# Keeping the expert gates of the last two token quarters on chip, and pinning the stores of the first two between the chunks

## The chip, the cores and the metric

One core of a Trainium2 chip (trn2) runs the whole program. The metric is the device time of one execution in microseconds; the time of a kernel is the median of its runs.

## The reference, cut to what matters

The program computes three transformer blocks over 256 tokens of width 1024. The change lies in the last sublayer, a product-key mixture of 16,384 experts (128 x 128):

```python
def _peer(h, w_query, sub_keys, expert_u, expert_v):
    q = (h @ w_query).reshape(B, S, PEER_HEADS, 2, PEER_KEY_DIM)
    sc = jnp.einsum('bshpk,hpnk->bshpn', q, sub_keys).astype(jnp.float32)
    v1, i1 = lax.top_k(sc[..., 0, :], PEER_TOPK)
    v2, i2 = lax.top_k(sc[..., 1, :], PEER_TOPK)
    ...
    top_s, pos = lax.top_k(cand, PEER_TOPK)
    idx = jnp.take_along_axis(cand_idx, pos, axis=-1)
    g = jax.nn.softmax(top_s, axis=-1).astype(h.dtype)
    ...
        u = expert_u[it]
        act = jax.nn.gelu(jnp.einsum('td,tkd->tk', xt, u))
        return jnp.einsum('tk,tkd->td', gt * act, expert_v[it])
```

Each token chooses 8 x 16 experts, each with a gate `g`. The reference gathers the rows of the chosen experts; the kernel does not gather.

## The kernel before

The kernel treats the sublayer densely: it computes the Gelu activation of all 16,384 experts for all 256 tokens, multiplies it with a gate matrix that is zero where an expert was not chosen, and multiplies the product with `expert_v`. An expert's number is 128 x its first key + its second; `n2` (0 to 127) is one second key, and a tile for one `n2` has the 128 first keys on the partitions and the 256 tokens along the free dimension.

The stages of `peer` around the change:

- `up(n2)` loads a slab of `expert_u` (512 KB, `raw`, by SP), splits it into a high part (`wH`, ScalarE, L268) and a rest (`wL`, VectorE, L270), runs 24 matmuls into a PSUM tile `acc` (two of these exist), and evicts it through Gelu on ScalarE (L1414), for most `n2` into a tile `gs`, which SP stores to a DRAM tensor `spill` (L1416); for the others into a kept tile `ga`. The `up` calls are independent of the routing and serve as filler for TensorE: `fill` issues them from a list while the routing and the gate build run.
- The gate build turns the chosen numbers and gates into the dense gate matrix, a quarter of the tokens (TQ = 64) at a time, four quarters, each in eight chunks of TC = 8 tokens. For a chunk VectorE makes one-hot tiles `A`, `eqb` and `Bg`, TensorE multiplies them (`gb`, 16 short matmuls, L1553), and ScalarE copies the result into `G` (L1554), a tile of 128 x 128 x 64 f32, 32 KB a partition, in two buffers. After a chunk, one store of the quarter before is popped from a list (`stores`), and `fill(2.8)` follows.
- A store writes an eighth of a quarter's `G` (512 KB) to the DRAM tensor `gd`, issued from ScalarE's queue (L1561, 32 in all). The stores of the last quarter follow between the remaining `up` calls.
- The expert loop runs over the 128 `n2`: `gates_of` loads gates of four `n2` from `gd` into `GG` (L1579, 512 KB, from SP, two groups ahead), VectorE multiplies activation and gate (`gw`, L1589), ScalarE and VectorE split the product (`gaH`, L1593; `gaL`, L1594), and 12 matmuls accumulate with the two parts of a slab of `expert_v` into four PSUM banks (`v`). Activations that were spilled are loaded back into `ga` (L1610).

The order of instructions on each engine is made by a planner, which simulates the program and issues what is ready first, in the order of priority in which the program was written; each engine then runs its list in order. `tc.keep_in_program_order(ins)` gives the planner an edge that puts `ins` behind the instruction written just before it on the same engine. SP issues nearly all loads; ScalarE issues the `gd` stores.

Of the kernel before, what the change touches and what calls it, by code (L numbers as in the profile page):

```python
# [11 lines left out]
F32 = mybir.dt.float32  # L12
# [5 lines left out]
AF = mybir.ActivationFunctionType  # L18
OP = mybir.AluOpType
# [200 lines left out]
def program(ctx: ExitStack, tc, I, out, co):  # L220
    nc = tc.nc
# [85 lines left out]
    def tables(name):  # L307

        tc.keep_in_program_order(nc.scalar.preload_act_table_set(name))
# [1062 lines left out]
    NQ = T // TQ  # L1372
# [6 lines left out]
    def peer(Xq, done):  # L1379
# [11 lines left out]
        X = normed(xt, 8, r, lambda k: cc("norm_ffn", k), pair())  # L1391
        pre.close()
        with pool("peer") as mp, pool("psp", 2, space=PS) as ps:
            iT = [mp.tile([128, T], F16 if j < 2 else F32, name=f"iT{j}") for j in range(3)]
            gp = [mp.tile([128, T], F16, name=f"gp{j}") for j in range(2)]
            iota = mp.tile([128, 128], F16, name="iota")
# [133 lines left out]

            done()

            gd = dram.tile([NQ, 128, 128, TQ], F32, name="gd")
            stores = []
            with pool("build") as bt, pool("psb", space=PS) as pb:
                for q in range(NQ):
                    G = bt.tile([128, 128, TQ], F32, name="G", bufs=2)
                    for c in range(TQ // TC):
                        A = bt.tile([128, TC, 128], F16, name="A", bufs=2)
                        B = bt.tile([128, TC, 2, 128], F16, name="Bg", bufs=2)  # L1540
                        s = slice(TQ * q + TC * c, TQ * q + TC * c + TC)
                        inner = lambda v: v[:, s, None].to_broadcast([128, TC, 128])
                        numbers = iota[:, None, :].to_broadcast([128, TC, 128])
                        eq = bt.tile([128, TC, 128], F16, name="eqb", bufs=1)
                        nc.vector.tensor_tensor(A, numbers, inner(iT[0]), op=OP.is_equal)
                        nc.vector.tensor_tensor(eq, numbers, inner(iT[1]), op=OP.is_equal)
                        for i in range(2):
                            nc.vector.tensor_tensor(B[:, :, i], eq, inner(gp[i]), op=OP.mult)
                        for j in range(0, TC, TP):
                            p = pb.tile([128, TP, 128], F32, name="gb", bufs=4)  # L1550
                            for k in range(TP):
                                for i in range(2):
                                    nc.tensor.matmul(p[:, k], A[:, j + k], B[:, j + k, i], start=i == 0, stop=i == 1)  # L1553
                            nc.scalar.activation(G[:, :, TC * c + j:TC * c + j + TP], p.rearrange("p t n -> p n t"), AF.Copy,  # L1554
                                                 scale=2.0 ** -15)
                        if stores:
                            stores.pop(0)()
                        fill(2.8)

                    def store(q, G, n):  # L1560
                        return lambda: nc.scalar.dma_start(gd[q, :, n:n + SN], G[:, n:n + SN])  # L1561

                    stores += [store(q, G, n) for n in range(0, 128, SN)]
                for n2 in todo:
                    up(n2)
                    if stores:
                        stores.pop(0)()
                while stores:
                    stores.pop(0)()
            with pool("psv", space=PS) as pv:  # L1570
                acc = [[pv.tile([128, 512], F32, name=f"v{t}{n}") for n in range(2)] for t in range(2)]
                with pool("gates") as gt:
                    parts = {}

                    def gates_of(i):

                        if i < 128 // GN:
                            parts[i] = gt.tile([128, NQ, GN, TQ], F32, name="GG", bufs=3)
                            dma(parts[i], gd[:, :, GN * i:GN * i + GN].rearrange("q n a t -> n q a t"))  # L1579

                    gates_of(0)
                    gates_of(1)
                    ends = []
                    for n2 in range(128):
                        h, j = divmod(n2, GN)
                        if j == 0:
                            gates_of(h + 2)
                        w = gt.tile([128, T], F32, name="gw", bufs=2)
                        nc.vector.tensor_tensor(w.rearrange("p (q t) -> p q t", q=NQ), ga.pop(n2).rearrange("p (q t) -> p q t", q=NQ),  # L1589
                                                parts[h][:, :, j], op=OP.mult)  # L1590
                        aH = gt.tile([128, T], F32R, name="gaH", bufs=2)
                        aL = gt.tile([128, T], F32R, name="gaL", bufs=2)
                        nc.scalar.activation(aH, w, AF.Copy)  # L1593
                        nc.vector.tensor_sub(aL, w, aH)  # L1594
                        H, L = slab(I["v"][n2])
                        ends.append((n2, (aH, aL), (H, L)))
                        if n2 == 126:
                            continue

                        order = (tc.keep_in_program_order,) if n2 == 127 else ()  # L1600
                        for t in range(2):
                            for n in range(2):
                                for m, a, b in ends:
                                    mm3(acc[t][n], [v[:, 128 * t:128 * t + 128] for v in a],
                                        [v[:, 512 * n:512 * n + 512] for v in b], m == 0, m == 127, *order)
                        ends.clear()
                        nxt = n2 + AHEAD
                        if nxt < STASH:
                            ga[nxt] = mp.tile([128, T], F32, name="ga", bufs=AHEAD)
                            dma(ga[nxt], spill[nxt - AHEAD])  # L1610
                        elif nxt < 128:
                            up(nxt)
                tables(LOGEXP)
                with pool("fin") as gt:
                    nf = gt.tile([128, D], F32, name="nf")
                    dma(nf, bass.AP(tensor=I["norm_final"].tensor, offset=I["norm_final"].offset, ap=[[0, 128], [1, D]]))
                    cs = [slice(512 * n, 512 * n + 512) for n in range(2)]
                    ss = [gt.tile([128, 2], F32, name="ss", bufs=2) for _ in range(2)]
                    rs = [gt.tile([128, 1], F32, name="rf", bufs=2) for _ in range(2)]
                    ys = [gt.tile([128, D], F32, name="y", bufs=2) for _ in range(2)]  # L1620
                    kept = tc.keep_in_program_order

                    def add(t, n):
                        xs = xtok[:, t, cs[n]]
                        kept(nc.vector.tensor_add(xs, acc[t][n], xs))
                        sq = gt.tile([128, 512], F32, name="sqf", bufs=2)
                        nc.scalar.activation(sq, xs, AF.Square, scale=D ** -0.5, accum_out=ss[t][:, n:n + 1])

                    def gain(t):
                        kept(nc.vector.tensor_mul(ys[t][:, cs[0]], xtok[:, t, cs[0]], nf[:, cs[0]]))  # L1630

                    def total(t):
                        kept(nc.vector.tensor_add(rs[t], ss[t][:, 0:1], ss[t][:, 1:2]))

                    def put(t, n):

                        kept(nc.vector.scalar_tensor_tensor(ys[t][:, cs[n]], xtok[:, t, cs[n]], rs[t], nf[:, cs[n]],
                                                            op0=OP.mult, op1=OP.mult))
                        dma(out[0, 128 * t:128 * t + 128, cs[n]], ys[t][:, cs[n]])

                    add(0, 0)
                    add(0, 1)
                    add(1, 0)
                    total(0)
                    gain(1)
                    add(1, 1)
                    rsqrt(rs[0], rs[0], gt, kept)
                    total(1)
                    put(0, 0)
                    put(0, 1)  # L1650
                    rsqrt(rs[1], rs[1], gt, kept)
                    nc.scalar.activation(ys[1][:, cs[0]], ys[1][:, cs[0]], AF.Copy, scale=rs[1])
                    dma(out[0, 128:, cs[0]], ys[1][:, cs[0]])
                    put(1, 1)
# [71 lines left out]
```

## Time and profile before

| | us |
|---|---|
| median of three timed runs | 2041.73 |
| lowest and highest of them | 2039.51, 2043.0 |
| the profiled execution, its own time | 2036.42 |
| its span, first to last instruction | 2034.6 |
| TensorE busy (PE) | 1933.5 (95%) |
| VectorE busy (DVE) | 1561.7 (77%) |
| ScalarE busy (ACT) | 1160.6 (57%) |
| GpSimd busy (POOL) | 116.0 (6%) |
| mean granted clock of TensorE, share of full speed | 0.975 |

The profile is of one execution. Its names: PE is TensorE, PEld its weight load, DVE VectorE, ACT ScalarE, SP the engine that only issues transfers; ACTq and SPq are the issue queues of ScalarE and SP. A line such as L1414 is the line of the kernel that issued the instruction; `out<-in` names its tiles. Times count from the start of the span. In this span the gate build runs from about 1389 to 1629 us, the hand-over to the expert loop until about 1669, the loop until about 2022, and the final normalization until the end.

### The profile page before, as it was taken

The page shows a single profiled execution, that of the slowest core. Times are in us where ns is not written, and L with a number is a line of the kernel's source. Part 1 is how long each engine was busy: PE and PEld are TensorE (multiplying, and loading weights), DVE is VectorE, ACT ScalarE, POOL GpSimd, SP SyncE. Part 2 cuts the span into 40 slices and gives each one's busy share as a digit, 9 for nine tenths or more (in the row PEclk, how much of TensorE's full clock was granted, in tenths as well). Part 3 has the DMA queues.
Part 4 walks back from the last instruction along what each step waited for, and adds up shares of the span by engine and source line. Part 5 has one row for each costly group of instructions (what it writes and reads, how often), then busy time and mean ns, then how long its engine had stood idle before and what let it go on. Part 6 is the DMA issues. An engine that isn't in the chain of part 4 may idle for free.

```text
span 2034.6 us, 36363 instructions
## 1 busy us (share of the span) xinstructions
PE 1933.5 (95%) x13516; PEld 1748.0 (86%) x13516; DVE 1561.7 (77%) x3040; ACT 1160.6 (57%) x2196; POOL 116.0 (6%) x139
## 2 busy tenths in 40 slices
PE   7988999989999999999999999999999989999998
PEld 6755899878888887999987999999999978888886
DVE  8877986466876877765687589999889847777676
ACT  5644586445775675774476464555444535555554
POOL 0000122120111102001000010000000000000000
PEclk9988999989999999999999999999999989999999
DMA  9775778676646535755643555556776688888774
GB/s 361 262 238 184 249 215 242 218 250 227 206 134 223 173 126 170 221 181 186 237 146 113 177 178 177 175 180 200 265 260 219 227 302 294 283 295 286 229 239 140
DMA packets 172434, 441.91 MB, mean 217 GB/s; under 512 B 21104, under 2 KB 75144, under 8 KB 171616
## 3 DMA queue, kind: packets, MB, share of 16 engines
q1 hardware_dynamic: 154608, 397.41, 59.4%
q10 hardware_dynamic: 11808, 36.70, 5.0%
q0 software_dynamic: 5840, 5.47, 1.1%
q8 instruction: 106, 1.74, 0.4%
q14 instruction: 72, 0.59, 0.1%
HBM read 398.40 MB, written 37.91 MB: 214 GB/s over the span
## 4 chain that ended last, share of the span: by engine, by line
PE 72%; DMA 12%; DVE 8%; issue 3%; ACT 3%; ACTq 1%; SPq 0%; POOL 0%; DVEq 0%; POOLq 0%
PE acc L275 16%; PE acc L276 16%; PE acc L277 16%; PE v L275 6%; PE v L276 6%; PE v L277 6%; DMA bias_d<-ob 5%; DMA araw<-in_adaT 4%; DVE wL L270 2%; DVE araw L465 1%; PE gb L1553 1%; ACTq L1561 1%; PE S L953 1%; DMA br<-buck_d 1%; ACT wH L268 1%
## 5 line engine op out<-in xcount | busy, mean ns | idle before, releaser
L270 DVE TENSOR_TENSOR wL<-raw,wH 128x1024 fp32r<-128x1024 f32 x565 | 695.0, 1232 | 242.5 <-ACT wH L268 224.4
L268 ACT ACTIVATE wH<-raw 128x1024 fp32r<-128x1024 f32 x565 | 596.9, 1059 | 489.3 <-PE acc L276 320.7
L275 PE MATMUL acc<-hH,wH 128*128 128x256 f32 (+1 forms) x2168 | 628.4, 290 | 29.4 <-ACT gs L1414 20.0
L276 PE MATMUL acc<-hL,wH 128*128 128x256 f32 (+1 forms) x2168 | 619.8, 286 | 3.2 <-DVE hL L394 3.2
L277 PE MATMUL acc<-hH,wL 128*128 128x256 f32 (+1 forms) x2168 | 619.1, 286 | 0.2 <-DVE wL L270 0.2
L275 PEld LDWEIGHTS acc<-hH,wH 128*128 128x128 f32 x2168 | 415.0, 191 | 39.4 <-ACT gs L1414 22.0
L276 PEld LDWEIGHTS acc<-hL,wH 128*128 128x128 f32 x2168 | 414.1, 191 | 7.6 <-DVE hL L394 4.1
L277 PEld LDWEIGHTS acc<-hH,wL 128*128 128x128 f32 x2168 | 413.9, 191 | 2.4 <-issue 1.0
L276 PE MATMUL v<-wL,gaH 128*128 128x512 f32 x512 | 199.2, 389 | 0.0
L275 PE MATMUL v<-wH,gaH 128*128 128x512 f32 x512 | 198.8, 389 | 0.0
L277 PE MATMUL acc<-hidH,wL 128*128 128x256 f32 x512 | 143.8, 281 | 0.0
L276 PE MATMUL acc<-hidL,wH 128*128 128x256 f32 x512 | 143.8, 281 | 0.0
L275 PE MATMUL acc<-hidH,wH 128*128 128x256 f32 x512 | 143.8, 281 | 0.0
L277 PE MATMUL v<-wH,gaL 128*128 128x512 f32 x512 | 141.3, 389 | 0.0
L465 DVE CUSTOM_DVE_ANT_0 araw<-araw,cond 128x1024 f32<-128x1024 f32 x72 | 88.7, 1234 | 37.5 <-DMA araw<-in_adaT 37.2
L277 PEld LDWEIGHTS v<-wH,gaL 128*128 128x128 f32 x512 | 96.1, 188 | 20.1
L275 PEld LDWEIGHTS v<-wH,gaH 128*128 128x128 f32 x512 | 96.1, 188 | 19.8
L276 PEld LDWEIGHTS v<-wL,gaH 128*128 128x128 f32 x512 | 96.1, 188 | 19.7
L1593 ACT ACTIVATE gaH<-gw 128x256 fp32r<-128x256 f32 x128 | 53.4, 418 | 104.1 <-PE v L276 93.9
L1594 DVE TENSOR_TENSOR gaL<-gw,gaH 128x256 fp32r<-128x256 f32 x128 | 54.3, 425 | 62.4 <-PE v L277 57.5
L275 PEld LDWEIGHTS acc<-hidH,wH 128*128 128x128 f32 x512 | 96.5, 189 | 1.3
L276 PEld LDWEIGHTS acc<-hidL,wH 128*128 128x128 f32 x512 | 96.5, 189 | 0.9
(447 smaller groups left out, 3273.8 us busy)
## 6 DMA issues: line engine op xcount, KB each, us to landing
raw<-in_w SPq DMA_DIRECT2D x128, 512.0 KB
raw<-in_uT SPq DMA_DIRECT2D x128, 512.0 KB
raw<-in_v SPq DMA_DIRECT2D x128, 512.0 KB
araw<-in_adaT SPq DMA_DIRECT2D x72, 512.0 KB
gd<-G ACTq DMA_DIRECT2D x32, 512.0 KB
GG<-gd SPq DMA_DIRECT2D x32, 512.0 KB
araw<-in_adaT ACTq DMA_DIRECT2D x24, 512.0 KB
raw<-in_w_dv SPq DMA_DIRECT2D x24, 512.0 KB
```

The source lines that it names most:

```text
L268: nc.scalar.activation(H, raw, AF.Copy)
L270: (lo or nc.vector).tensor_sub(L, raw, H)
L275: kept(nc.tensor.matmul(p, aH, bH, start=start, stop=False))
L276: kept(nc.tensor.matmul(p, aH, bL, start=False, stop=False))
L277: kept(nc.tensor.matmul(p, aL, bH, start=False, stop=stop))
L465: nc.vector.tensor_tensor_reduce(raw, raw, cond, scale=1.0, scalar=0.0, op0=OP.mult, op1=OP.add, accum_out=MOD[l][:, j:j + 1])
L953: nc.tensor.matmul(Ss[i][:, t], pm(q[rows], t), kt, start=True, stop=True)
L1553: nc.tensor.matmul(p[:, k], A[:, j + k], B[:, j + k, i], start=i == 0, stop=i == 1)
L1561: return lambda: nc.scalar.dma_start(gd[q, :, n:n + SN], G[:, n:n + SN])
L1593: nc.scalar.activation(aH, w, AF.Copy)
L1594: nc.vector.tensor_sub(aL, w, aH)
```

## The change

`G` becomes one tile with two halves, kept until the expert loop is done; quarter `q` is built in half `q % 2`. Only the first two quarters are stored to DRAM, so that `gd` and `GG` shrink to half; the last two overwrite their halves and stay. Sixteen stores are left. Each is pinned by `tc.keep_in_program_order`, and after the chunks 1 and 4 of a quarter two are popped instead of one, so that a quarter's eight are out after chunk 5. The product `gw` of an `n2` is made by two VectorE instructions of 128 tokens each, the first with gates from `GG`, the second straight from `G` (a pattern of two runs of 64, 32 KB apart). The pops behind the build are gone, since nothing is left to store there.

```diff
--- before.py
+++ after.py
@@ -1391,6 +1391,7 @@
         X = normed(xt, 8, r, lambda k: cc("norm_ffn", k), pair())
         pre.close()
         with pool("peer") as mp, pool("psp", 2, space=PS) as ps:
+            keep_stack = ExitStack()
             iT = [mp.tile([128, T], F16 if j < 2 else F32, name=f"iT{j}") for j in range(3)]
             gp = [mp.tile([128, T], F16, name=f"gp{j}") for j in range(2)]
             iota = mp.tile([128, 128], F16, name="iota")
@@ -1530,11 +1531,13 @@
 
             done()
 
-            gd = dram.tile([NQ, 128, 128, TQ], F32, name="gd")
+
+            gd = dram.tile([2, 128, 128, TQ], F32, name="gd")
+            keep = keep_stack.enter_context(pool("keep"))
+            G = keep.tile([128, 2, 128, TQ], F32, name="G")
             stores = []
             with pool("build") as bt, pool("psb", space=PS) as pb:
                 for q in range(NQ):
-                    G = bt.tile([128, 128, TQ], F32, name="G", bufs=2)
                     for c in range(TQ // TC):
                         A = bt.tile([128, TC, 128], F16, name="A", bufs=2)
                         B = bt.tile([128, TC, 2, 128], F16, name="Bg", bufs=2)
@@ -1551,22 +1554,20 @@
                             for k in range(TP):
                                 for i in range(2):
                                     nc.tensor.matmul(p[:, k], A[:, j + k], B[:, j + k, i], start=i == 0, stop=i == 1)
-                            nc.scalar.activation(G[:, :, TC * c + j:TC * c + j + TP], p.rearrange("p t n -> p n t"), AF.Copy,
+                            nc.scalar.activation(G[:, q % 2, :, TC * c + j:TC * c + j + TP], p.rearrange("p t n -> p n t"), AF.Copy,
                                                  scale=2.0 ** -15)
-                        if stores:
-                            stores.pop(0)()
+                        for _ in range(2 if c in (1, 4) else 1):
+                            if stores:
+                                stores.pop(0)()
                         fill(2.8)
 
-                    def store(q, G, n):
-                        return lambda: nc.scalar.dma_start(gd[q, :, n:n + SN], G[:, n:n + SN])
-
-                    stores += [store(q, G, n) for n in range(0, 128, SN)]
+                    def store(q, n):
+                        return lambda: tc.keep_in_program_order(nc.scalar.dma_start(gd[q, :, n:n + SN], G[:, q, n:n + SN]))
+
+                    if q < 2:
+                        stores += [store(q, n) for n in range(0, 128, SN)]
                 for n2 in todo:
                     up(n2)
-                    if stores:
-                        stores.pop(0)()
-                while stores:
-                    stores.pop(0)()
             with pool("psv", space=PS) as pv:
                 acc = [[pv.tile([128, 512], F32, name=f"v{t}{n}") for n in range(2)] for t in range(2)]
                 with pool("gates") as gt:
@@ -1575,7 +1576,7 @@
                     def gates_of(i):
 
                         if i < 128 // GN:
-                            parts[i] = gt.tile([128, NQ, GN, TQ], F32, name="GG", bufs=3)
+                            parts[i] = gt.tile([128, 2, GN, TQ], F32, name="GG", bufs=3)
                             dma(parts[i], gd[:, :, GN * i:GN * i + GN].rearrange("q n a t -> n q a t"))
 
                     gates_of(0)
@@ -1586,8 +1587,9 @@
                         if j == 0:
                             gates_of(h + 2)
                         w = gt.tile([128, T], F32, name="gw", bufs=2)
-                        nc.vector.tensor_tensor(w.rearrange("p (q t) -> p q t", q=NQ), ga.pop(n2).rearrange("p (q t) -> p q t", q=NQ),
-                                                parts[h][:, :, j], op=OP.mult)
+                        act = ga.pop(n2).rearrange("p (q t) -> p q t", q=NQ)
+                        for q, g in ((0, parts[h][:, :, j]), (2, G[:, :, n2])):
+                            nc.vector.tensor_tensor(w.rearrange("p (q t) -> p q t", q=NQ)[:, q:q + 2], act[:, q:q + 2], g, op=OP.mult)
                         aH = gt.tile([128, T], F32R, name="gaH", bufs=2)
                         aL = gt.tile([128, T], F32R, name="gaL", bufs=2)
                         nc.scalar.activation(aH, w, AF.Copy)
@@ -1610,6 +1612,7 @@
                             dma(ga[nxt], spill[nxt - AHEAD])
                         elif nxt < 128:
                             up(nxt)
+                keep_stack.close()
                 tables(LOGEXP)
                 with pool("fin") as gt:
                     nf = gt.tile([128, D], F32, name="nf")
```

## Rows read from the trace of the kernel before

**Rows 1.** Busy time by stretch: stretch, length, busy time (instructions), clock, DMA, GB/s.
```profile
1389.00:1449.00 60.00, 60.00 (x561) 59.24 (x560) 55.64 (x49) 32.04 (x52) 0.00 (x0) 1.00 0.61 205
1449.00:1479.00 30.00, 26.43 (x248) 25.52 (x248) 27.50 (x25) 13.87 (x23) 0.00 (x0) 1.00 0.84 298
...
1509.00:1539.00 30.00, 26.33 (x237) 25.58 (x235) 26.58 (x24) 14.10 (x23) 0.00 (x0) 0.94 0.83 304
...
1629.00:1669.00 40.00, 31.65 (x214) 30.39 (x213) 14.35 (x17) 14.90 (x24) 0.00 (x0) 0.87 0.86 314
1669.00:2022.00 353.00, 353.00 (x1604) 294.11 (x1603) 263.15 (x379) 189.52 (x258) 0.00 (x0) 1.00 0.79 258
sum 633.00, PE 612.15 PEld 547.49 DVE 495.04 ACT 323.49 POOL 0.00; mean PE 68.02 PEld 60.83 DVE 55.00 ACT 35.94 POOL 0.00
```

**Rows 2.** Waits of TensorE, 1380 to 1670: us in total, times, longest.
```profile
PE acc L275 <- ACT gs L1414: 20.0, 10, 4.1
PE gb L1553 <- DVE Bg L1548: 0.8, 1, 0.8
```

**Rows 3.** Chain of waits, 1624 to 1662, the store issues: start, us.
```profile
1625.27 0.35 ACTq L1561
1625.66 0.45 ACTq L1561
...
1626.66 1.60 ACTq L1561
```

**Rows 4.** All instructions on tile gd, the stores: duration min/median/max in ns.
```profile
L1561 ACTq DMA_DIRECT2D gd<-G x32: 326/1157/2013, 1448.7 to 1632.0; - x32
```

**Rows 5.** Timeline of ScalarE, first and last burst: start, us, [idle before].
```profile
1454.16 0.38 ACT L1414 ACTIVATE gs<-acc 128x256 f32<-128x256 f32 x1 [5.45 <-issue]
...
1633.34 0.66 ACT L1414 ACTIVATE gs<-acc 128x256 f32<-128x256 f32 x2 [8.10 <-issue]
```

**Rows 6.** Timeline of TensorE, where it waited.
```profile
1454.60 0.39 PE L275 MATMUL acc<-hH,wH 128*128 128x256 f32 x1 [1.47 <-ACT gs L1414]
...
1633.78 0.58 PE L275 MATMUL acc<-hH,wH 128*128 128x256 f32 x1 [4.10 <-ACT gs L1414]
...
1643.67 0.39 PE L275 MATMUL acc<-hH,wH 128*128 128x256 f32 x1 [1.30 <-ACT gs L1414]
...
1652.54 0.39 PE L275 MATMUL acc<-hH,wH 128*128 128x256 f32 x1 [2.95 <-ACT gs L1414]
```

**Rows 7.** Busy time in the four stretches at the lower clock.
```profile
1516.80:1520.20 3.40, 3.40 (x18) 3.40 (x18) 0.61 (x1) 2.08 (x3) 0.00 (x0) 0.51 1.02 419
...
1632.80:1639.70 6.90, 5.92 (x28) 5.92 (x29) 2.36 (x2) 3.16 (x5) 0.00 (x0) 0.51 1.03 412
1653.30:1656.70 3.40, 3.40 (x18) 3.40 (x18) 0.24 (x1) 0.00 (x0) 0.00 (x0) 0.50 1.05 391
sum 17.10, PE 16.12 PEld 16.03 DVE 5.29 ACT 8.32 POOL 0.00; mean PE 4.03 PEld 4.01 DVE 1.32 ACT 2.08 POOL 0.00
```

**Rows 8.** Timeline of TensorE, 45 matmuls apart at full clock.
```profile
1644.01 0.28 PE L277 MATMUL acc<-hH,wL 128*128 128x256 f32 x1
...
1649.32 0.28 PE L277 MATMUL acc<-hH,wL 128*128 128x256 f32 x1
```

**Rows 9.** Timeline of ScalarE at the hand-over.
```profile
1652.11 0.75 ACT L1414 ACTIVATE gs<-acc 128x256 f32<-128x256 f32 x2 [0.59 <-DMA spill<-gs]
```

**Rows 10.** Groups of instructions, 1200 to 2035: names, shapes, xcount | us, ns | idle.
```profile
L1589 DVE TENSOR_TENSOR gw<-ga,GG 128x256 f32<-128x256 f32 x128 | 54.1, 424 | 5.6 <-DMA GG<-gd 1.3
...
L1490 DVE TENSOR_TENSOR got<-got,su 128x128 f32<-128x128 f32 x2 | 0.6, 287 | 0.0
```

**Rows 11.** Timeline of VectorE in the expert loop.
```profile
1682.15 0.42 DVE L1594 TENSOR_TENSOR gaL<-gw,gaH 128x256 fp32r<-128x256 f32 x1 [0.47 <-PE v L277]
```

**Rows 12.** Busy time over the whole gate build.
```profile
1389.00:1629.00 240.00, 227.50 (x2101) 222.99 (x2100) 217.54 (x189) 119.06 (x194) 0.00 (x0) 0.99 0.69 237
```

**Rows 13.** Waits of SP's queue, 1380 to 1700.
```profile
SPq L1416 <- DMA gd<-G: 14.4, 3, 7.1
```

## The prediction

> **What bounds the kernel now.** I read the busy time by stretch first, because an average over the whole program would hide the edited stage. From 1669 to 2022 us, the loop over the 128 expert rows that multiplies with `expert_v`, TensorE is busy all the time at full clock [rows 1]: nothing to win there, whatever happens to transfers. In the gate build, and in the hand-over after it, TensorE is idle for 633.00 - 612.15 = 20.85 us, always right after a quarter of the tokens is finished: 3.57 us after the first, 3.67 after the second, 5.26 after the third (20.85 less the other three), 8.35 after the last. While the first quarter is built, with no store in the queues yet, it is never idle [rows 1].
>
> The waits say what ends that idle time: 20.0 us of it is TensorE waiting for ScalarE's Gelu eviction `gs` (L1414), and 0.8 us VectorE's `Bg` [rows 2]. Only two `acc` tiles exist, so TensorE can fill one more and must then wait. The chain of waits shows why ScalarE is late: the eight stores `gd<-G` of a quarter are issued back to back from its queue, and while it issues, it evicts nothing [rows 3]. The program spreads them one per chunk of eight tokens; the order on ScalarE did not keep that. The first store of a burst takes 0.35 us to issue, the second 0.45, later ones up to 1.60, about what 0.52 MB takes at the 412 GB/s that the DMA engines then move (1.3 us) [rows 3, 7]; the median of all 32 is 1.157 and the largest 2.013 [rows 4]. ScalarE's timeline gives the hold before the next `gs`: 5.45 us in the first burst, 8.10 in the last [rows 5]. TensorE then waited 1.47 and 4.10 us [rows 6]. The difference is 4.0 us both times: a hold of up to about 4 us costs nothing. The rest of each burst's idle time follows some 10 us later, when the delayed evictions come in pairs.
>
> The idle time has a second price. Four times in or right after these waits the granted clock is 0.50 to 0.51, the 1.2 GHz level, for 17.10 us in all, in which TensorE was busy for 16.12 us [rows 7]. At that level 28 matmuls took 5.92 us, 211 ns each [rows 7]; at full clock 45 of them (L277 at 1644.01 to L277 at 1649.32) took 5.31 us, 118 ns each [rows 8]. So 1 - 118 / 211 = 0.44 of 16.12 us, or 7.1 us, is lost. Everything that a perfect feed could give back is 20.85 + 7.1 = 28.0 us.
>
> **The change part by part.** *Stores of the last two quarters* go away: 16 issues of the 32, and 8.4 MB written. The bursts behind 1569 and 1629 vanish with nothing in their place. Their idle time is 5.26 + 8.35 = 13.6 us; three of the four slow-clock stretches (all but the first) are behind them, 13.70 us long, 12.72 us busy, 5.6 us lost [rows 7]. Together 19.2 us.
>
> *Stores of the first two quarters* stay, but each is pinned behind the eviction traced before it, so at most two stand together, in chunks 1 and 4, and all eight are out by chunk 5. A single one holds ScalarE for about 0.35 us, a pair 0.35 + 0.45 = 0.8 us [rows 3]. The upper bound is twice the largest issue, 4.0 us [rows 4]: still what the second `acc` tile absorbs. I take 0.8, since a chunk lasts about 60 / 8 = 7.5 us and each store finds the queue empty, like the first of a burst. So these two bursts give back 3.57 + 3.67 us and the first slow stretch, 3.40 x 0.44 = 1.5: another 8.7 us.
>
> A rule of the Trainium skill speaks about this term (DMA: Bandwidth & Descriptors, section Issuing engines are not separate DMA queues): issuing from several engines saves only the sequencer's issue time, which it calls usually small relative to the transfer. The first two issues of a burst agree with it; the fourth takes 1.60 us, more than the transfer itself. By the rule alone the hold would be too small to matter, and the transferred bytes would be the cause: rival one below.
>
> *One `G` of 64 KB a partition* replaces two buffers of 32 KB; the third quarter overwrites the first one's half. It needs the landing of all eight stores, the last issued two chunks, about 15 us, earlier; before, the same reuse waited for a burst. I put it at nothing; a late landing would cost its lateness, twice.
>
> *Gates loads `GG`* halve to 256 KB. They are prefetched two groups of four experts ahead under a busy TensorE [rows 1], so: nothing in the loop. At the hand-over it helps: a `gs` waited there for a `spill` landing [rows 9], behind a first product that waited 1.3 us for `GG` [rows 10]; TensorE lost 2.95 us to that `gs` [rows 6], already in the 8.35. `GG` can now be late only by its own load, since the last store that it reads is issued in chunk 5 of the third quarter.
>
> *The product `gw`* becomes two instructions of 128 columns. One of 256 takes 424 ns, a product of 128x128 of the same type 287 [rows 10]. Halves without any fixed part would add nothing; two of 287 add 150 ns per expert, 128 x 150 = 19.2 us of VectorE work, and I take that, as the size is the same. What hides it: VectorE waits 0.47 us per expert for TensorE to free a `gaL` buffer [rows 11], so 0.32 us are left over. Queued behind the second product are the next `wL` and `gaL`, and both stay ahead of TensorE. If that cover were gone, the full 19 us would show.
>
> The Trainium skill argues against splitting (VectorE: DVE Perf Modes, section on the TRN2 errata): a fixed latency per SBUF instruction, so tiles should be large. Its (N + 151) / 0.96 would make this an estimated 20.1 us of VectorE time; the rows say 19.2, and by both it stays under TensorE's time.
>
> **Sum.** 28.0 us, less what I expect to remain: the 0.8 us wait for `Bg`, and the 1.30 us wait for `gs` at 1643.67, which has no store just ahead of it [rows 2, 6]. That is 25.9, say 26. The profiled execution took 2036.42 us (span 2034.6 plus 1.8), so 2010.4 in its terms. The three timed runs have a median of 2041.73, 5.3 us above it; I carry this over: 2041.7 - 26 = 2015.7.
>
> **Rivals.**
> 1. *The bytes stall TensorE, not the issues.* Then the first two bursts' 8.7 us stay and only 19.2 are won: 2022.5. For it: in the slow stretches the DMA share is above 1.0 [rows 7]. Against: the wait equals the hold less 4.0 us at both ends [rows 5, 6]. This is the rule of the page on DMA put to work. Chance 0.10.
> 2. *VectorE becomes the bound of the build.* It is busy 217.54 of 240 us there [rows 12], against 227.50 for TensorE, some 224.5 at full clock. With the dependency gaps of the unstalled first quarter (55.64 busy of 60.00) it needs 217.54 / 0.927 = 234.7 us: 5.3 won in the build, plus the hand-over's 8.35 and 4.1 (5.92 + 3.40 us busy at the slow clock, times 0.44 [rows 7]): 17.8 won, or 2024. Against: in that quarter TensorE is at 100% all the same [rows 1]. Chance 0.10.
> 3. *Slower: pinned stores wait on ScalarE for a landing.* An issue can wait for another transfer's landing before it goes: SP's `spill` stores did, for `gd` stores, up to 7.1 us [rows 13]. If all 16 pinned stores were held 7.1 us, each would cost 7.1 - 4.0 = 3.1, together 50, less the 28 won: 2064. It turns the sign from 4.0 + 28 / 16 = 5.75 us per store. Against: the waits on SP came three times in all, with the queues full of a burst. Chance 0.04.
> 4. *The planner, given another graph, orders the stage anew and puts the stalls elsewhere.* Anything from no change to a small gain: within 4 us of before, 2041, chance 0.04; between 4 and 14 won, some 2033, chance 0.04.
>
> **How the numbers follow.** My forecast, 24 to 28 us won, has 0.68. About 0.2% (4 us) is what timing can tell from no change. Faster: 0.68 + 0.10 + 0.10 + 0.04 = 0.92; same 0.04; slower 0.04. The range starts at 28 us and a fast set of runs (2.2 us under the median), 2011, and reaches past rivals one and two to 2025; about 0.15 lies outside.
>
> **What would show it.** Right: 16 `gd<-G` issues, none with more than one neighbour, medians near 0.35 us; no wait of TensorE for `gs` above 1.5 us before the hand-over; full clock from 1389 us to the end of the loop; span near 2008.6. Rival one: waits for `gs` under short holds. Rival two: TensorE waiting for `Bg` or `wL` again and again. Rival three: ScalarE idle before a store. What would make me wrong outright: `gw` pairs far above 574 ns, or TensorE below 100% in the expert loop.

## The result, and the profile after

The changed kernel took 2018.37 us (median of 4 runs, 2016.35 to 2022.32), the kernel before 2040.62 beside it (4 runs, 2035.52 to 2043.0): a ratio of 0.9893, with a 95% interval of 0.9871 to 0.9915. It is faster by 22.3 us; 26.0 was forecast, and 2018.37 lies in the range given. A second measurement gave 2018.26 against 2039.82 (0.9883, 0.9866 to 0.9901).

Lines of the changed kernel have moved: the eviction `gs` is L1415, the eviction of `G` L1557, the stores L1565, the loads of `GG` L1580, `gw` L1592, `gaH` L1595, `gaL` L1596. First TensorE's waits from 1380 to 2010 us in the changed kernel (us in total, times, longest), which answer to [rows 2]:

```profile
PE v L275 <- ACT gaH L1595: 5.9, 1, 5.9
```

The ten waits for `gs`, 20.0 us, and the one for `Bg` are gone. One wait is left, of a kind that the list of before does not have: the first product of the expert loop. The busy time by stretch of the changed kernel, in the columns of [rows 1], shows where it lies:

```profile
1402.00:1639.50 237.50, 237.50 (x2214) 234.65 (x2212) 218.75 (x190) 127.64 (x206) 0.00 (x0) 1.00 0.71 235
1639.50:1652.00 12.50, 6.55 (x21) 5.11 (x20) 4.56 (x14) 3.39 (x6) 0.00 (x0) 0.73 0.69 218
1652.00:2003.00 351.00, 351.00 (x1595) 292.52 (x1594) 270.20 (x500) 189.11 (x258) 0.00 (x0) 1.00 0.75 237
```

The gate build, from the first eviction of `G` to the last, is without a gap and at full clock; so is the loop. All 5.95 us of idle time stand in the 12.50 us between them. The stores of the changed kernel, as in [rows 4], and ScalarE around the pair in chunk 1, as in [rows 5]:

```profile
L1565 ACTq DMA_DIRECT2D gd<-G x16: 326/327/500, 1456.5 to 1559.5; - x16
```

```profile
1464.51 0.36 ACT L1415 ACTIVATE gs<-acc 128x256 f32<-128x256 f32 x1
1464.79 0.60 ACT L1557 ACTIVATE G<-gb 128x512 f32<-128x512 f32 x1
1465.19 0.33 ACTq L1565 DMA_DIRECT2D gd<-G  x1
1465.28 0.59 ACT L1557 ACTIVATE G<-gb 128x512 f32<-128x512 f32 x1
1465.56 0.45 ACTq L1565 DMA_DIRECT2D gd<-G  x1
```

The median issue fell from 1157 ns to 327, the longest from 2013 to 500. No eviction stands behind more than two issues.

Now the hand-over. The chain of waits of the changed kernel (start, us, what) goes from the last matmuls of the build over a load of gates to the first product:

```profile
1637.96 0.69 PE gb L1556 x13
1638.65 6.37 DMA GG<-gd
1645.05 0.30 DVE gw L1592
1645.37 0.42 ACT gaH L1595
1645.84 0.80 PE v L275
```

The load starts when the last `gb` matmul ends, and among the waits of SP's queue from 1380 to 1700 us stands one for just that:

```profile
SPq L1580 <- PE gb L1556: 0.2, 1, 0.2
```

It is so although the last of all the stores was issued at 1559.5, 79 us earlier. TensorE still had `acc` matmuls until 1639.90 and then nothing. At the end of the wait and behind it the clock is at its 1.2 GHz level for 6.8 us (the clock column, 0.50):

```profile
1644.00:1650.80 6.80, 4.96 (x12) 3.94 (x13) 2.33 (x9) 1.24 (x3) 0.00 (x0) 0.50 0.64 212
```

By the 0.44 of the prediction this costs 4.96 x 0.44 = 2.2 us. The hand-over so costs 5.95 + 2.2 = 8.2 us. In the kernel before, 8.35 idle and 4.1 at the low clock were lost there.

### The profile page after: what moved, and what is told of

Same layout as the page of the kernel before. It is cut to its first block, busy times and chain, and to the rows that moved or that the text cites. A ratio compares the mean times of both kernels' runs of the same rounds, so it can differ in the third digit from the quotient of the medians.

```text
span 2016.2 us, 36483 instructions
## 1 busy us (share of the span) xinstructions
PE 1927.8 (96%) x13516; PEld 1744.0 (86%) x13516; DVE 1568.6 (78%) x3168; ACT 1160.5 (58%) x2196; POOL 115.8 (6%) x139
## 4 chain that ended last, share of the span: by engine, by line
PE 74%; DMA 12%; DVE 8%; issue 3%; ACT 3%; ACTq 0%; SPq 0%; DVEq 0%
PE acc L275 16%; PE acc L276 16%; PE acc L277 16%; PE v L275 6%; PE v L276 6%; PE v L277 6%; DMA bias_d<-ob 5%; DMA araw<-in_adaT 5%; DVE wL L270 2%; PE gb L1556 1%; DVE araw L465 1%; ACT wH L268 1%; PE S L953 1%; PE acc L936 1%; DVE araw L485 1%
## 5 line engine op out<-in xcount | busy, mean ns | idle before, releaser
L1595 ACT ACTIVATE gaH<-gw 128x256 fp32r<-128x256 f32 x128 | 53.4, 417 | 110.9 <-PE v L276 97.4
L1596 DVE TENSOR_TENSOR gaL<-gw,gaH 128x256 fp32r<-128x256 f32 x128 | 54.4, 425 | 66.4 <-PE v L277 61.8
```

## The experiments

Nine kernels, each beside runs of the kernel before on the same chip (medians there 2041.97, 2039.82 and 2041.53 for the three groups). Two executions of one kernel can differ by some 7 us in how long they take to come to the edited stage (last section). So the table also gives a stretch within the profile: from the start of the first eviction of `G` to the start of the last `xtok<-v,xtok`, the addition behind the last product. In the kernels that keep `G` on chip the profile shows 3847 or 3848 TensorE instructions in it; in the three that do not, 3902. Counted in `acc` matmuls alone, 1869 against 1808 (some records of `gb` are missing from the profiles), it is 61 more: the work of two and a half `up` products, at 118 ns each some 7.2 us, which the kernels that keep `G` do before the stretch. Where the two sorts are compared, that is to be taken off.

| kernel | median us | ratio to before (95%) | stretch us |
|---|---|---|---|
| before | 2040.62 | 1 | 635.5 |
| changed | 2018.37 | 0.9893 (0.9871 to 0.9915) | 606.3 |
| changed, without the pins | 2026.82 | 0.9926 (0.9906 to 0.9946) | 614.6 |
| before, pins alone | 2033.85 | 0.9962 (0.9947 to 0.9977) | 628.2 |
| before, stores issued by GpSimd | 2026.70 | 0.9918 (0.9895 to 0.9941) | 619.5 |
| changed, first two `GG` in own memory | 2015.72, again 2014.25 | 0.9873 (0.9855 to 0.9891), 0.9871 (0.9856 to 0.9886) | 599.7, 599.7 |
| changed, once more | 2018.26 | 0.9883 (0.9866 to 0.9901) | 604.6 |
| changed, two groups of four | 2013.84 | 0.9870 (0.9854 to 0.9885) | 600.0 |
| changed, one group of eight | 2029.21 | 0.9945 (0.9931 to 0.9959) | 615.1 |
| groups of four and own memory | 2014.46 | 0.9863 (0.9842 to 0.9884) | 600.2 |
| changed, `gw` in four | 2016.99 | 0.9875 (0.9854 to 0.9895) | 603.9 |

**Without the pins.** The changed kernel, half of its stores gone, but those that stay not pinned:

```diff
-  return lambda: tc.keep_in_program_order(nc.scalar.dma_start(gd[q, :, n:n + SN], G[:, q, n:n + SN]))
+  return lambda: nc.scalar.dma_start(gd[q, :, n:n + SN], G[:, q, n:n + SN])
```

> The changed kernel without the pins: the last two quarters' gates stay on chip, and the 16 stores that are left may float. Hold theory (the issue of stores in a row keeps ScalarE from evicting, about 4 us of it free): bursts of eight come back behind the first two quarters, ACTq issues with a median above 1 us, TensorE waits some 3.6 us for gs after each, with a slow-clock stretch now and then; 7 to 9 us slower than the changed kernel, about 15 us faster than before. Rival (halving the bytes did it, the pins do nothing): no wait for gs, the time of the changed kernel, 22 us faster than before.

It took 2026.82 us, 8 more than the changed kernel, and its stretch is as much longer. Its ScalarE at the second quarter's stores, and TensorE's waits from 1380 to 2020:

```profile
1508.34 7.65 ACTq L1565 DMA_DIRECT2D gd<-G  x7
1516.03 0.38 ACT L1415 ACTIVATE gs<-acc 128x256 f32<-128x256 f32 x1 [7.73 <-issue]
1516.09 1.18 ACTq L1565 DMA_DIRECT2D gd<-G  x1
```

```profile
PE acc L275 <- ACT gs L1415: 7.9, 4, 4.2
PE gb L1556 <- DVE Bg L1551: 3.5, 3, 2.0
```

The bursts are back, and with them the waits: a hold of 7.73 us, a wait of 4.25. The planner also put the rest differently: ten `gs` evictions lie behind the last `G` eviction here and one in the changed kernel, so there is no wait at the hand-over. The pins' own worth in the build is therefore more than the 8 us: 7.9 + 3.5 us of waits and 10.2 us at the 1.2 GHz level (8.8 of them busy, some 3.9 lost) are some 15, against which the changed kernel loses 8.2 at its hand-over. The expectation of 7 to 9 us did not count this second part, so it came right partly by luck.

**The pins alone.** The kernel before, all 32 stores and all bytes, each store pinned, still one per chunk:

```diff
-  return lambda: nc.scalar.dma_start(gd[q, :, n:n + SN], G[:, n:n + SN])
+  return lambda: tc.keep_in_program_order(nc.scalar.dma_start(gd[q, :, n:n + SN], G[:, n:n + SN]))
```

> The kernel before with its 32 stores pinned one per chunk and nothing kept on chip, so no byte less. Hold theory: no wait of TensorE for gs while the four quarters are built (12.5 us of idle time and some 3 us of slow clock gone); the last quarter's eight stores still go out in a row behind the build, and the expert loop waits for them and for its first GG load, at least the 12 us that the hand-over cost before; 8 to 16 us faster than before. Rival (bytes are the cost): the waits after each quarter stay near 3.6 us and the time stays within 4 us of before.

TensorE's waits from 1380 to 2020, the stretch of the hand-over, and what stands in it on the queues and on VectorE:

```profile
PE v L275 <- ACT gaH L1593: 19.5, 1, 19.5
```

```profile
1640.70:1661.00 20.30, 2.14 (x5) 1.77 (x6) 2.22 (x7) 0.77 (x3) 0.00 (x0) 0.58 0.98 363
```

```profile
1640.75 9.56 ACTq L1561 DMA_DIRECT2D gd<-G  x8
1647.69 3.15 SPq L1579 DMA_DIRECT2D GG<-gd  x3
1657.93 0.76 DVE L1589 TENSOR_TENSOR gw<-ga,GG 128x256 f32<-128x256 f32 x2 [17.21 <-DMA GG<-gd]
```

In the build TensorE waits for `gs` not once and its clock does not fall, with not a byte less to move. The whole remaining loss is the last quarter: its stores go out in a row at the end, 9.56 us, and the first load of gates waits for them. So the two halves of the change do different things: the pins cure the build, and keeping the last quarters takes the stores out of the hand-over.

**Stores issued by GpSimd.** The kernel before, same stores and bytes, but none in ScalarE's queue:

```diff
-  return lambda: nc.scalar.dma_start(gd[q, :, n:n + SN], G[:, n:n + SN])
+  return lambda: nc.gpsimd.dma_start(gd[q, :, n:n + SN], G[:, n:n + SN])
```

> The kernel before with its 32 stores issued from GpSimd's queue, floating as before: the same bytes in the same bursts, and ScalarE issues none. Hold theory: no wait of TensorE for gs behind the first three quarters, 12 to 24 us faster than before. Rival (bytes saturate the DMA engines, and late loads or late spill stores stall TensorE): the waits after each quarter stay, above 3 us each, and the time stays within 4 us of before.

TensorE's waits of this kernel for `gs` from 1380 to 2020, two lines of ScalarE's waits from 1380 to 1700, and the stores:

```profile
PE acc L275 <- ACT gs L1414: 9.6, 8, 2.0
```

```profile
ACT gs L1414 <- DMA spill<-gs: 11.7, 10, 2.5
ACT wH L268 <- DMA raw<-in_uT: 3.4, 3, 2.0
```

```profile
L1561 POOL DMA_DIRECT2D gd<-G x32: 531/533/586, 1458.2 to 1633.0; - x32
```

15 us are won by moving the issues alone. The waits of 4 us are gone. Half of the 20.0 us stays, in short waits: four in the build, 5.5 us with the longest at 2.05, and four at the hand-over. So the hold theory's time came out, but not its absence of waits. Ahead of some of them ScalarE itself waits, for `spill` stores to land and free a buffer of `gs`, or for late loads. In the kernel before it waited 0.6 us for `spill`, and with the same bytes one store at a time (the pins alone) 0.4. So the bytes have a price too where the stores go out together. That all of the 9.6 us come from it is not shown: ahead of the three waits of 1.3 us at the hand-over no such wait stands.

The issue itself behaves differently here: in bursts of eight too, each of the 32 took GpSimd 0.53 to 0.59 us, where ScalarE's took up to 2.0 [rows 4].

**GG in memory of its own.** The changed kernel, with the first two `GG` tiles in the pool of `G`:

```diff
-  parts[i] = gt.tile([128, 2, GN, TQ], F32, name="GG", bufs=3)
+  parts[i] = (keep if i < 2 else gt).tile([128, 2, GN, TQ], F32, name="GG", bufs=2 if i < 2 else 3)
```

> The changed kernel with the first two GG tiles in memory of their own instead of memory that the build's one-hot tiles used. Theory of the hand-over: the first GG load waits there for the last gb matmul to free that memory, and no up is left to cover its 6.4 us; with its own memory it is loaded during the third or fourth quarter, TensorE's wait of 5.9 us for gaH shrinks to about 1.5 us (the last G eviction, gw and gaH in a row), the slow-clock stretch behind it goes, and the kernel is 5 to 8 us faster than the changed one (2011 to 2013). Rival (the wait is the chain from the last gates to the first product, or the spill reloads, and GG only came last by a little): TensorE still waits 4 us or more there and the time stays within 3 us of the changed kernel.

> The first two GG tiles in memory of their own again, now timed on the chip of the others. Theory of the hand-over (GG waits there for memory that the build's tiles hold): the wait at the hand-over is 1.6 us instead of 5.9 and there is no slow clock behind it, 4.3 + 2.3 = 6.6 us; the last look by profiles gave 5.6 and by medians 2.7, so 3 to 6.6 us faster than the changed kernel on this chip, 2011.5 to 2015. Rival (the wait is shorter but what follows runs later by as much): within 2 us of the changed kernel.

TensorE and ScalarE run the same instructions in the same order as in the changed kernel. The loads of `GG`, and the first product of the loop, in the first of the two executions:

```profile
L1580 SPq DMA_DIRECT2D GG<-gd x32: 370/371/557, 1525.6 to 1960.1; - x32
```

```profile
1642.56 0.50 PE L275 MATMUL v<-wH,gaH 128*128 128x512 f32 x1 [1.61 <-ACT gaH L1595]
```

The first load starts at 1525.6, 113 us earlier than in the changed kernel. The wait shrinks from 5.95 to 1.61 us and the low clock behind it is gone. What made the load late was memory: in the changed kernel `GG` is laid where the build's one-hot tiles were, and these are read by the last `gb`. The stretch is 6.6 us shorter than in the changed kernel's first profile and 4.9 than in its second. The medians differ by 2.7, less than the 5 to 8 expected, and by 4.0 where both were timed on one chip; in both comparisons the intervals of the ratios overlap, so the gain rests on the wait and the stretch more than on the medians. The 1.61 us that stay are a queue: `gaH` stands on ScalarE behind the eviction of the last filler product.

The changed kernel once more, on the chip of the second group:

> The changed kernel unaltered, for the comparison with the three beside it: 2018 us by both theories, within the 2016 to 2022 seen before, with a wait of about 6 us at the hand-over and none of over 0.5 us on gs between the first G and it.

```profile
PE v L275 <- ACT gaH L1595: 3.6, 1, 3.6
```

It took 2018.26 us. The wait at the hand-over was 3.6 us, not the 6 expected: the same load, again released by the last `gb`, took 4.04 us instead of 6.37. With 2.7 us for the low clock behind it, the hand-over cost 6.3 us here. So its cost differs from one execution to the next.

**Groups of four.** The changed kernel, pops changed:

```diff
-  for _ in range(2 if c in (1, 4) else 1):
+  for _ in range(4 if c in (1, 4) else 0):
```

> Pinned in two groups of four instead of six of one or two. Theory of the hold (four issues in a row cost ScalarE about 0.35 + 0.45 + 1.1 + 1.1 = 3.0 us, below the 4 us that the waits seen before were shorter than their holds): no wait on gs in the build, time of the changed kernel within 2 us. Rival (the distance matters, each group costs its hold less the buffers' slack of one or two products): four waits of 1 to 3 us, 4 to 12 us slower.

All of TensorE's waits from 1380 to 2020, one group of stores with the eviction behind it, and VectorE's wait for the load:

```profile
PE acc L275 <- ACT gs L1415: 1.3, 1, 1.3
```

```profile
1553.26 0.33 ACTq L1565 DMA_DIRECT2D gd<-G  x1
1553.62 3.41 ACTq L1565 DMA_DIRECT2D gd<-G  x3
1557.16 0.38 ACT L1415 ACTIVATE gs<-acc 128x256 f32<-128x256 f32 x1 [3.21 <-issue]
```

```profile
1642.39 0.49 DVE L1592 TENSOR_TENSOR gw<-ga,GG 128x128 f32<-128x128 f32 x2 [1.16 <-DMA GG<-gd]
```

Both expectations missed, since both looked only at the build. There the theory nearly held: holds of 2.6 to 3.9 us (1553.26 to 1557.16 is the longest), and one wait of 1.3 us instead of none. But the kernel is 4 us faster than the changed one (the intervals of the ratios overlap; the stretch is 4.6 to 6.3 us shorter), for a reason outside the build: the planner left more `up` work behind the last `gb`. TensorE goes on until the first product at 1644.42, while the load, issued at 1639.47 and still in the reused memory, comes at 1642.39. VectorE waits for it, TensorE does not.

**One group of eight.** The same line with `range(8 if c == 1 else 0)`.

> All eight stores of a quarter pinned in one group behind chunk 1. Theory of the hold: eight issues in a row hold ScalarE for about 8 us, as the burst of 8.10 us in the kernel before, which gave a wait of 4.1 us; two such groups, so two waits of about 4 us and slow clock behind them at some 1.2 us each: 8 to 12 us slower than the changed kernel, 2026 to 2030. Rival (the pins cured the build by the place of the stores against the evictions of gs, not by their spacing): no wait over 1.5 us and within 2 us of the changed kernel.

ScalarE's queue, and TensorE's wait behind it, at the second group, then all of TensorE's waits from 1380 to 2020:

```profile
1526.05 0.33 ACTq L1565 DMA_DIRECT2D gd<-G  x1
1526.41 8.87 ACTq L1565 DMA_DIRECT2D gd<-G  x7
```

```profile
1535.83 0.58 PE L275 MATMUL acc<-hH,wH 128*128 128x256 f32 x1 [5.62 <-ACT gs L1415]
```

```profile
PE acc L275 <- ACT gs L1415: 12.0, 4, 5.6
PE gb L1556 <- DVE Bg L1551: 1.6, 1, 1.6
```

2029.21 us, 11 slower than the changed kernel on this chip, within the range of the theory of the hold. A pin as such cures nothing: what counts is how many issues the pins leave in a row. The size came out partly by luck: the build lost 13.6 us in waits and some 3.5 at the low clock, more than the 10.4 that the expectation counts, while the hand-over, with ten evictions of `gs` left to cover it, lost nothing, where the changed kernel lost 6.3. The free part of a hold is not the same everywhere either. ScalarE was idle for 8.64 us before the next `gs` here, which is 3.0 more than TensorE's wait; in this kernel's other group it was 8.27 and 3.53, or 4.7 more.

**Both cures of the hand-over.** Groups of four and `GG` in own memory.

> Groups of four and the first two GG tiles in memory of their own, together. Theory of the hand-over (what TensorE waits there is the load of GG and the two operations behind it, less the products that are left to cover them): in the groups of four 5 us of products were left and the wait was already gone, so memory of its own has nothing more to give but the 1.3 us of gw on VectorE that nobody waited for: within 2 us of the groups of four alone, 2012 to 2016, with no wait at the hand-over, or one of up to 1.6 us if fewer products are left there. Rival (the two gains are separate and add): 3 to 4 us faster than either, 2010.

TensorE's waits from 1380 to 2020:

```profile
PE acc L275 <- ACT gs L1415: 1.9, 2, 1.3
```

No wait at the hand-over, 2014.46 us, a stretch of 600.2 against 600.0 and 599.7 for either alone. The gains do not add: both take away the same wait.

**`gw` in four.** The changed kernel, with 64 columns at a time:

```diff
-  nc.vector.tensor_tensor(w.rearrange("p (q t) -> p q t", q=NQ)[:, q:q + 2], act[:, q:q + 2], g, op=OP.mult)
+  for d in range(2):
+      nc.vector.tensor_tensor(w.rearrange("p (q t) -> p q t", q=NQ)[:, q + d], act[:, q + d], g[:, d], op=OP.mult)
```

> The gate multiplication of the changed kernel in four operations of 128x64 per expert instead of two of 128x128. From 424 ns at 128x256 and some 287 at 128x128, one of 128x64 is estimated at 215 to 220 ns, so 0.29 us more per expert on VectorE. Theory (the split is hidden by the 0.47 us that VectorE waits for TensorE in every expert): VectorE's wait shrinks to 0.18 us or so, TensorE still runs at 100% in the loop, time of the changed kernel within 2 us (2016 to 2020). Rival (VectorE's chain is what sets the pitch of 2.72 us): 0.1 to 0.29 us for each of some 125 experts, 13 to 36 us slower.

VectorE in the loop of the changed kernel:

```profile
1762.78 0.42 DVE L1596 TENSOR_TENSOR gaL<-gw,gaH 128x256 fp32r<-128x256 f32 x1 [0.47 <-PE v L277]
1763.23 0.29 DVE L1592 TENSOR_TENSOR gw<-ga,GG 128x128 f32<-128x128 f32 x1
1763.44 0.28 DVE L1592 TENSOR_TENSOR gw<-ga,G 128x128 f32<-128x128 f32 x1
1763.80 1.23 DVE L270 TENSOR_TENSOR wL<-raw,wH 128x1024 fp32r<-128x1024 f32 x1
```

And with four:

```profile
1762.28 0.36 DVE L1593 TENSOR_TENSOR gw<-ga,GG 128x64 f32<-128x64 f32 x2
1762.56 0.35 DVE L1593 TENSOR_TENSOR gw<-ga,G 128x64 f32<-128x64 f32 x2
1762.85 1.23 DVE L270 TENSOR_TENSOR wL<-raw,wH 128x1024 fp32r<-128x1024 f32 x1
1764.54 0.42 DVE L1597 TENSOR_TENSOR gaL<-gw,gaH 128x256 fp32r<-128x256 f32 x1 [0.47 <-PE v L277]
```

No change in time (2016.99), TensorE busy throughout the loop. But the wait for TensorE did not shrink from 0.47 us to 0.18 as expected. From the first `gw` to the start of `wL` it is 0.57 us with two instructions and with four: 1763.80 - 1763.23 and 1762.85 - 1762.28. Successive instructions overlap, so their durations do not add.

## Why the prediction came out as it did

*What bounds the kernel, and the stores.* Right. The bursts' 3.57 + 3.67 + 5.26 us in the build, with their low clock, are gone, and no `gs` wait remained; the pins alone did it with all the bytes in place. Of 17.10 us at the low clock in four stretches [rows 7], 6.8 us in one, at the hand-over, are left; the sign "full clock from 1389 us to the end of the loop" failed there.

*The free 4 us of a hold.* Right as a size, not as a constant. By the prediction's own measure it is 4.0 us in the two bursts that it read, 3.7 (5.98 held, 2.25 waited) and 3.85 (7.00, 3.15) in the other two of the kernel before, 3.5 in the kernel without pins (7.73, 4.25), 3.0 and 4.7 in the groups of eight. Holds of 2.6 to 3.9 us in the groups of four cost 1.3 us in all.

*Rival one, the bytes.* Wrong as the cause: with all bytes and the pins, TensorE waits for `gs` nowhere. But the shift of the issues to GpSimd shows that the bytes of a whole burst are not free either: part of the 9.6 us of short waits there stands behind late transfers. The rule of the Trainium skill behind that rival (DMA: Bandwidth & Descriptors, section Issuing engines are not separate DMA queues) is that issuing from several engines saves only issue time, usually small beside the transfer. This case's runs agree that issue time is what was saved, but not that it is small: moving the issues won 15 us, a ratio of 0.9918, since an issue late in a burst took some 1.2 us of an engine that others wait for.

*Rival two, VectorE as the bound of the build.* Wrong: TensorE was busy in 237.50 of 237.50 us beside VectorE's 218.75. *Rival three, a pinned store that waits for a landing*: none; the longest issue was 500 ns. *Rival four, the planner's new order*: no stall in the build, but the rival had the right agent. The order did change, and what it cost lies at the hand-over.

*`gw` in two.* Hidden, as predicted, but the term was too large: VectorE's busy time in 351 us is 270.20, against 263.15 in 353 before [rows 1], at equal length some 66 ns per expert and not 150, because the two overlap by 80 ns (1763.23 + 0.29 against 1763.44). Even this is not seen in the chain, as the `gaL` wait is still 0.47 us [rows 11]: the kernel before had 0.15 us between the end of `gw` and the start of `wL` (1764.62 to 1764.77 in its timeline), and the second instruction took that gap.

The Trainium skill's (N + 151) / 0.96 (VectorE: DVE Perf Modes, section on the TRN2 errata) gives an estimated 291 ns for 128 columns and 224 for 64; the runs show 283 to 291 and 218 to 221, so for single durations the trace agrees. As a cost per added instruction the formula is too high here, since 66 ns is what one added.

*`GG` at the hand-over.* This step failed. The prediction said that `GG` "can now be late only by its own load". It followed the data, the stores that the load reads, and forgot the memory that the load writes. With `G` kept, the next tiles lie in what the build's one-hot tiles leave, and that is free only at the last `gb`; that they lay in the freed buffers of `G` before is likely, but no run shows it. A second thing came with it: the planner put more filler into the build. Ten `gs` evictions stood behind the last eviction of `G` before, one stands there now. Over all the runs this goes with the stores: nine or ten are left in the four kernels that have bursts of eight stores in the build, none to two in the others. It seems, then, that the cure of the build used up what had covered the hand-over; why the planner does so was not tried. Thus 6.37 us of load and 0.7 of operations had 1.25 us of TensorE work to hide behind.

*The sum.* Forecast was a remainder of 2.1 us out of 28.0; 8.2 remained, all of it at the hand-over. By rows that is 12.5 us of idle time won in the build, 8.35 - 5.95 = 2.4 at the hand-over and 7.1 - 2.2 = 4.9 of low clock: 19.8. The medians show 22.3, and the stretch, with the 7.2 us taken off, 635.5 - 7.2 - 606.3 = 22.0. Of the 2.2 us between it and the rows, 1.2 lie behind the last product, where the prediction had no term. In the kernel before, the last matmul of the last product started at 2025.16 and its `xtok` at 2026.81, 1.65 us later, since two instructions of the normalization stood ahead of it on VectorE:

```profile
2026.12 0.16 DVE L1633 TENSOR_TENSOR rf<-ss 128x1 f32<-128x1 f32 x1 [1.20 <-ACT sqf L1627]
2026.20 0.69 DVE L1630 TENSOR_TENSOR y<-xtok,nf 128x512 f32<-128x512 f32 x1
```

In the changed kernel that `xtok` followed 0.43 us after the start of that matmul (2007.87):

```profile
2008.30 0.69 DVE L1628 TENSOR_TENSOR xtok<-v,xtok 128x512 f32<-128x512 f32 x1
```

The last 1.0 us is not placed. So the forecast of 26.0 is as near as it is partly by luck: 6.1 us more than expected remained, and 2.2 that it did not count came in. With the late load cured, the difference was 2039.82 - 2014.25 = 25.6 us, close to what was forecast for the change.

Faster, then, for the reason given; the term that was mis-sized is the remainder, put at 2.1 us and measured at 8.2 (6.3 in the second profile).

## What to carry to other kernels

In this kernel a transfer issued from an engine's queue was work of that engine: count how many issues stand in a row before an instruction that others wait for, and pin them apart if the planner may gather them. When a buffer is kept longer, look for the tile that used to be laid in its place: it goes to other memory, and its first load waits for the last reader there. And after a change in the order, check what filler is left to cover the next start-up.

## What was not expected of the hardware

From ScalarE's queue an issue took longer the more of them stood just ahead: stores of 0.52 MB took 0.33 us alone, 0.44 to 0.50 as the second of a pair in the changed kernel (up to 0.65 in its second profile), and 1.1 to 1.3 us each on average in rows of seven (7.65 and 8.87 us for seven). From GpSimd's queue the same stores took 0.53 to 0.59 us each, the eighth in a row no more than the first.

An added VectorE instruction cost far less than its duration: 64-column products of 218 to 221 ns started 0.14 us apart (two of them end 0.36 us after the first starts), and four took 0.57 us in all, as long as two of 128 columns.

The same program reaches the edited stage at different times. The evictions of `G` in the two profiles of the changed kernel:

```profile
L1557 ACT ACTIVATE G<-gb x64: 582/597/616, 1402.0 to 1638.9; 128x512 f32<-128x512 f32 x64
```

```profile
L1557 ACT ACTIVATE G<-gb x64: 581/596/618, 1409.1 to 1646.0; 128x512 f32<-128x512 f32 x64
```

They start 7.1 us apart and take 236.9 us in both. That is a third of what the change gave, and the reason why differences of 3 us are read here within a stretch.
